# The table of TensorE durations by which a kernel orders its own instructions

## The chip, the cores and the metric

The kernel runs on one core of a Trainium2 chip. The metric is the time of one execution on the device in microseconds (us); the smaller the better. The core has a TensorE for products (PE in the profile, with PEld for its weight loads), a VectorE (DVE), a ScalarE (ACT), a GpSimd (POOL) and a SyncE (SP), each of which works off its own queue of instructions in the order in which they were put there. Products are written to banks of PSUM, everything else lies in SBUF.

## What is computed

Two blocks of a language model on x of 512 tokens by 1024 features, in fp32. What stands around the change is the first half of the first block and the window attention of the second:

```
h = rms_norm(x);  q, k, v, glu_a, glu_b = split(h @ w_in)
q, k = rms_norm over the 64 features of each of 8 heads
z = q . k / 8;  log_one_minus = where(s < t, log_sigmoid(-z), 0)
tail = reversed cumsum(log_one_minus) - log_one_minus
attn = where(s < t, exp(log_sigmoid(z) + tail), 0) @ v        # "stick breaking"
c = glu_a * sigmoid(glu_b);  c = causal depthwise convolution, 31 taps
c = silu(layer_norm(c));  x = x + concat(attn, c) @ w_out
x = x + (silu(conv3(h @ w_gate)) * (h @ w_val)) @ w_down       # 2816 wide
second block: gated linear attention (4 heads), attention in a window of 128
  with 8 heads of 64 features and 2 of keys, w_out, a feed-forward as above, rms_norm
```

## The kernel before

All operands of the large products are split into two float32r (f32r) parts, hi and lo, so that a product of fp32 accuracy is three f32r products (`mm3`): hi by hi, hi by lo, lo by hi. `WeightStream` loads the weights in chunks on SP's queue (`raw`), casts each on ScalarE (`whi25` is that of chunk 25, 128x1024) and takes the rest on VectorE (`wlo25`). The scores of both attentions are true fp32 products of 64 rows: the two heads of a pair lie in rows 0 to 63 and 64 to 127 of one tile. The trace shows an fp32 product as two records.

**The order is made by the kernel itself.** The body is written stage by stage, in the order of `ORDER1` ("glu0 glu1 k1 taps2 taps0 k0 q0 v conv0 stick0 q1 conv2 stick1 cnorm stick2 wo0 stick3 wo1 wo2 wo3") and `ORDER2`, but `rec.engine("PE")` and its like hand out proxies that only record the instruction (class `Recorder`, from line 42). `Recorder.order` (from line 154) then plays the whole program through with a table of durations, `Recorder.cost` (from line 111): an engine that comes free takes the first instruction in program order whose operands are there by then. `issue` (line 257) emits the instructions in the order of the starts thus found. So each queue's order is fixed when the kernel is built, and line 266 stands for nearly all of them in the profile. A tile belongs to a lane with a fixed number of buffers (`BUFS`), taken in program order. A copy on `ANY` goes to ScalarE or VectorE, whichever is free first in that play.

Names that return below: `q1ps0` and `q1ps1` are the two banks of the q projection of heads 4 to 7 (96 f32r products of 256 columns), `q1tn`, `q1sq`, `q1u`, `q1r` their norm on ScalarE. In `stick_pair(j)` (from line 687) heads 2j and 2j+1 have three banks of scores each (`z2_0` is head 2, bank 0): bank 0 with 256 and 128 columns, bank 1 with 384, bank 2 with 512. After the scores and a mask product, `softplus` makes `e` from a bank by Abs, Exp and Ln on ScalarE and splits it into `sph` and `spl`; products of these with triangles and blocks of -1 (`con_r`) are added onto the scores, here called sums; a last Exp from the bank gives the weights, which go into the products `av`. The convolution's first 14 taps of a pair of tiles are products by ScalarE, summed by accumulating DMAs on POOL's queue (`tap<-tap`); tap tiles share the lane x with the `e` tiles. `conv_norm` takes the mean (`cmu`) and the variance (`cvar`) by products, then `cln_u` and `crstd`, and silu in place on `conv`; its results `c_hi`, `c_lo` are the operands of the first output products `wo`. The feed-forwards (products `g`, `u`, `d`) follow. In the second block `aq` are projections for the window attention, `avT` the transposes of its values.

Of the kernel before, what the change touches and what calls it, by code (L numbers as in the profile page):

```python
# [9 lines left out]
F32R = mybir.dt.float32r  # L10
# [5 lines left out]
P = 128  # L16
# [17 lines left out]
class Op:  # L34
    """One recorded instruction."""

    def __init__(self, index, queue, method, args, kw):
        self.index, self.queue, self.method, self.args, self.kw = index, queue, method, args, kw
        self.columns = None
        self.needs, self.then, self.first, self.ready, self.end = 0, [], [], 0.0, 0.0  # L40


class Recorder:
    """Records the instructions of a kernel, orders them by list scheduling and issues them in that order.

    An engine takes, whenever it is free, the first instruction in program order whose operands are
    there; tiles of a lane are taken in program order, each when one of its buffers is free.
    """

# [6 lines left out]
    SWITCH = 40  # L56
    COPY = {"ANY": ("ACT", "DVE")}
# [56 lines left out]
    def cost(self, op, queue, out, ins):  # L114
        n = 1
        for d in out.shape[1:]:
            n *= d
        pointers = sum(1 for a in ins if a.shape[-1] == 1 and len(a.shape) == 2 and n > 1)
        op.set = None
        if op.method == "dma_start":  # L120
            op.bytes = 4 * n * out.shape[0]
            return {"SP": 450.0, "ACT": 450.0, "POOL": 1040.0}[queue]
        if queue == "PE":
            if op.method == "transpose":
                return n / 1.2 + 2
            if out.shape[0] <= 64:
                first = out.offset // out.ap[0][0]
                op.columns = frozenset(range(first, first + out.shape[0], 32))
            passes, m = (1, ins[0].shape[-1]) if ins[0].dtype == F32R else (4, 2 * ins[0].shape[-1])
            return max(passes * n / 2.4 + 2.6, m / 1.2)  # L130
        if queue == "ACT":
            func = next((a.name for a in op.args if isinstance(a, AF)), op.kw.get("func"))
            op.set = self.SETS.get(func)
            return n / 1.2 + (50 if ins[0].space == bass.MemoryType.PSUM else 93) + 93 * pointers \
                + (93 if "accum_out" in op.kw else 0)
        if queue == "POOL":
            return n / 0.96 + 60
        fast = op.method in ("copy", "tensor_copy", "tensor_scalar", "tensor_scalar_add", "tensor_scalar_mul", "memset")
        sbuf = all(a.space != bass.MemoryType.PSUM for a in [out] + ins)
        if op.method == "tensor_reduce":  # L140
            n = 1
            for d in ins[0].shape[1:]:
                n *= d
        return n / (1.92 if fast and sbuf else 0.96) + 67 + 62 * pointers

    def hop(self, a, b):
        """From the end of `a` to the earliest start of `b`, which needs it."""
# [6 lines left out]
    def order(self):  # L154
        """The instructions in the order of their starts, with the table sets to load before them."""
        free = {q: 600.0 for q in self.engines}
# [7 lines left out]
        drained, columns = 0.0, None  # L164
# [5 lines left out]
        def admit(op):  # L170
            """Operands are there: waits for its tiles, in the order of their lanes, then is offered."""
# [18 lines left out]
        while len(result) < len(self.ops):  # L190
# [35 lines left out]
            if q == "PE":  # L226
                while when >= (window + 1) * self.WINDOW:
# [41 lines left out]
class WeightStream:  # L269
    """Loads weight chunks in the order of use and splits each into two float32r parts."""  # L270
# [38 lines left out]
def weight_plan():  # L309
    """Chunks of the weights in the order of use: key, input, rows of 128 from and count, columns."""  # L310
# [87 lines left out]
def kernel(  # L398
# [70 lines left out]
    def minus_sums(src, name):  # L469
        """Minus the sums over the partitions, in each partition."""  # L470
# [7 lines left out]
    def rsqrt(ps, scale, r, name):  # L478
        """r = 1 / sqrt(scale * ps + eps): by logarithm, then one Newton step."""
# [8 lines left out]
    class Norm:  # L488
        """Parts of g * x for the products, and 1 / rms(x) by token."""
# [45 lines left out]
    def mm3(ps, w, xx, first, last):  # L535
        """ps += w.T @ x for operands given as two float32r parts each."""
# [4 lines left out]
    def project(w, m, xs, name, tag="mm"):  # L541
        """Feature-major [128 features, 512 tokens] tile m of the chunk."""
# [9 lines left out]
    def project_tok(tag, keys, xs, name):  # L552
        """Token-major [128 tokens, 512 features] tiles, all four."""
# [39 lines left out]
    cpad = []  # L593

    def glu(c):
        """By token, then by channel, with 30 zeros before the first token."""
# [39 lines left out]
    def project_quarter(keys, name, tag="mm"):  # L636
        """Token-major [128 tokens, 256 features] halves of two banks, all four."""
# [11 lines left out]
    def qk_quarter(which, c):  # L649
        """Four heads: norm over the 64 features of a head, then by feature."""  # L650
# [34 lines left out]
    BANKS = [[(2, 0), (3, 256)], [(1, 0)], [(0, 0)]]  # L685

    def stick_pair(j):
        """Two heads, scores as [s, t]: blocks of 128 positions s from the last to the first.

        log of a weight is z[s, t] - sum over s <= j < t of softplus(z[j, t]); the sums over j are  # L690
        products with triangles and blocks of -1, added to the scores where they lie.
        """
# [65 lines left out]
    def conv_taps(j0):  # L758
        """First taps of two tiles: products by ScalarE, sums by accumulating DMA."""
# [31 lines left out]
    def conv_norm():  # L791
        """Layer norm over the channels and silu."""
# [29 lines left out]
    def mixer_out(key, part, mixs, cs=range(4), norm=None, gain=None, x_in=None):  # L822
        """Columns cs; onto the tiles x_in, if given, else onto xT; norm takes the sums."""
# [71 lines left out]
    # lower bounds of the forget gates: first row of the softmax over the two rows  # L895
# [29 lines left out]
    # ================ second block ================  # L925
# [26 lines left out]
    def hg_scores(js):  # L952
        """Decayed scores q_t . k_s prod(f_{s+1..t}) of the heads js, [s, t] by tile pairs.

        ks holds k_s times the forget gates after s in its block, qp holds q_t times the gates
        of its block up to t, tot their product over each block; blocks double level by level.
        """
# [146 lines left out]
    def swa_pair(j):  # L1104
        """Two heads of one group of keys and values, side by side."""
# [36 lines left out]
        # by key: block b of itself, then block b of the next block of queries  # L1142
# [42 lines left out]
    # residual by token  # L1185
# [18 lines left out]
    def final_half(t):  # L1204
        """Sum of squares of the first half of the features; that half times its gain."""
# [7 lines left out]
    def final_part(t, cols):  # L1213
        """Adds the squares of some features of the second half."""
# [48 lines left out]
def _masks(np):  # L1263
    """Identity, level masks of the doubling, window mask; identity, triangles, blocks of -1."""
# [33 lines left out]
```

## Time and profile before

| | |
|---|---|
| runs | 1208.17, 1208.4, 1210.71 us (median 1208.4) |
| span of the profiled execution | 1205.9 us |
| median less that span | 2.5 us |
| TensorE busy | 1191.8 us, 99% |
| VectorE, ScalarE, GpSimd busy | 761.3, 504.1, 32.4 us |

The profiled execution is known by its span alone; the profile gives no other time for it. An engine is busy while it has an instruction under way; that TensorE's products follow without a gap does not say that they are needed when they run. So the table is read beside the list of waits: where TensorE waits, and what it waits for.

### The profile page before, as it was taken

The numbers are of one execution on the slowest core, as the hardware profiler recorded it, in microseconds if no ns is written. First come the engines' busy times: TensorE is split into PE (matmuls) and PEld (weight loads), VectorE is DVE, ScalarE is ACT, GpSimd is POOL, SyncE is SP. The second block draws the span as 40 slices with busy tenths as digits, with TensorE's granted clock in tenths as the row PEclk, the third lists the DMA queues.
The fourth block names the chain that finished last, engine by engine and source line by source line (L and its number), as shares of the span: only waits on it lengthen the run. The fifth ranks groups of instructions, "written<-read, shape, count | busy, mean of one in ns | idle before, by whom it ended". The sixth has DMA issues, their size and how long they took to land.

```text
span 1205.9 us, 15657 instructions
## 1 busy us (share of the span) xinstructions
PE 1191.8 (99%) x6144; PEld 988.7 (82%) x6144; DVE 761.3 (63%) x1288; ACT 504.1 (42%) x795; POOL 32.4 (3%) x85
## 2 busy tenths in 40 slices
PE   9999999999999999999999999999999999999997
PEld 8998766888888888888889877778888888888886
DVE  6889885676653566355775667877666445653554
ACT  7286796453321233133544245655523223321324
POOL 0033100000000000000000000000000000000000
PEclk9999999999999999999999999999999999999999
DMA  7389421233232323322322222112332323232321
GB/s 235 106 181 200 92 88 35 77 99 105 88 105 88 105 90 103 92 96 79 118 70 72 70 78 68 49 61 79 105 100 92 104 89 105 88 105 89 103 71 70
DMA packets 36553, 116.09 MB, mean 96 GB/s; under 512 B 4224, under 2 KB 4352, under 8 KB 36480
## 3 DMA queue, kind: packets, MB, share of 16 engines
q1 hardware_dynamic: 31248, 105.65, 28.1%
q0 software_dynamic: 4512, 8.39, 4.0%
q8 instruction: 48, 0.79, 0.3%
q10 hardware_dynamic: 720, 1.05, 0.2%
q14 instruction: 25, 0.20, 0.1%
HBM read 105.12 MB, written 2.10 MB: 89 GB/s over the span
## 4 chain that ended last, share of the span: by engine, by line
PE 94%; DMA 3%; DVE 1%; ACT 1%; issue 0%; SPq 0%; ACTq 0%; POOLq 0%
PE d L266 20%; PE g L266 20%; PE u L266 20%; PE wo L266 7%; PE z L266 4%; DMA tap<-tap 2%; PE hi L266 2%; PE glub L266 2%; PE hg L266 2%; PE glua L266 2%; PE hq L266 2%; PE hf L266 2%; PE aq L266 2%; PE hl L266 2%; PE av L266 1%; PE k0ps L266 1%
## 5 line engine op out<-in xcount | busy, mean ns | idle before, releaser
L266 ACT CAST whi<-raw 128x1024 fp32r<-128x1024 f32 (+2 forms) x194 | 200.8, 1035 | 475.2 <-PE d L266 152.1
L266 DVE TENSOR_TENSOR wlo<-raw,whi 128x1024 fp32r<-128x1024 f32 (+2 forms) x194 | 233.0, 1201 | 93.7 <-ACT whi L266 93.4
L266 PE MATMUL g<-n_hi,whi 128*128 128x512 f32 x352 | 137.2, 390 | 0.0
L266 PE MATMUL g<-n_hi,wlo 128*128 128x512 f32 x352 | 137.1, 390 | 0.0
L266 PE MATMUL g<-n_lo,whi 128*128 128x512 f32 x352 | 137.1, 389 | 0.0
L266 PE MATMUL u<-n_lo,whi 128*128 128x512 f32 x352 | 137.0, 389 | 0.0
L266 PE MATMUL u<-n_hi,whi 128*128 128x512 f32 x352 | 137.0, 389 | 0.0
L266 PE MATMUL u<-n_hi,wlo 128*128 128x512 f32 x352 | 137.0, 389 | 0.0
L266 PEld LDWEIGHTS u<-n_hi,whi 128*128 128x128 f32 x352 | 66.1, 188 | 13.8
L266 PEld LDWEIGHTS u<-n_hi,wlo 128*128 128x128 f32 x352 | 66.1, 188 | 13.7
L266 PEld LDWEIGHTS g<-n_hi,wlo 128*128 128x128 f32 x352 | 66.1, 188 | 13.7
L266 PEld LDWEIGHTS g<-n_hi,whi 128*128 128x128 f32 x352 | 66.1, 188 | 13.7
L266 PEld LDWEIGHTS u<-n_lo,whi 128*128 128x128 f32 x352 | 66.1, 188 | 13.6
L266 PEld LDWEIGHTS g<-n_lo,whi 128*128 128x128 f32 x352 | 66.1, 188 | 13.5
L266 DVE TENSOR_TENSOR s<-s,u 128x512 f32<-128x512 f32 x44 | 30.3, 688 | 67.1 <-PE u L266 67.1
L266 DVE TENSOR_TENSOR gp<-g,n__rstd 128x512 f32<-128x512 f32 x44 | 30.4, 692 | 63.9 <-PE g L266 63.8
L266 PE MATMUL d<-wlo,f_hi 128*128 128x512 f32 (+1 forms) x182 | 69.5, 382 | 0.0
L266 PE MATMUL d<-whi,f_lo 128*128 128x512 f32 (+1 forms) x182 | 69.5, 382 | 0.0
L266 PE MATMUL d<-whi,f_hi 128*128 128x512 f32 (+1 forms) x182 | 69.5, 382 | 0.0
L266 PE MATMUL d<-f_hi,whi 128*128 128x512 f32 x176 | 68.5, 389 | 0.0
L266 PE MATMUL d<-f_lo,whi 128*128 128x512 f32 x176 | 68.5, 389 | 0.0
L266 PE MATMUL d<-f_hi,wlo 128*128 128x512 f32 x176 | 68.5, 389 | 0.0
(389 smaller groups left out, 2388.6 us busy)
## 6 DMA issues: line engine op xcount, KB each, us to landing
raw<-in_weights_dram SPq DMA_DIRECT2D x182, 512.0 KB, 3.6
tap<-tap POOLq DMA_DIRECT2D x30, 256.0 KB, 4.7
raw<-in_weights_dram SPq DMA_DIRECT2D x8, 384.0 KB, 3.1
xin<-in_x_dram SPq DMA_DIRECT2D x8, 256.0 KB, 6.2
xres<-in_x_dram SPq DMA_DIRECT2D x8, 256.0 KB, 3.4
raw<-in_weights_dram SPq DMA_DIRECT2D x4, 256.0 KB, 5.7
out_dram<-hts ACTq DMA_DIRECT2D x4, 256.0 KB, 2.8
out_dram<-hts SPq DMA_DIRECT2D x4, 256.0 KB, 2.6
```

The costliest lines, as they stand in the source:

```text
L266: getattr(self.engines[op.queue], method)(*op.args, **op.kw)
```

## The change

Three things change in the durations by which `order` plays the program. An f32r product now takes 13.6 ns over its columns at 2.4 per ns (before 2.6), or 4 ns over the columns of its weights at 1.2 per ns, whichever is more; an fp32 product counts as two passes. A product of 64 rows or fewer may now stand beside another on other rows, as one with 64 outputs or fewer could before on other columns. And whenever the shape changes (64 rows or not, 64 outputs or not), 110 ns are added. Comments and docstrings went too, so that line 266 is now line 276. No operation differs.

```diff
+    DRAIN = 110.0
...
             if op.method == "transpose":
                 return n / 1.2 + 2
-            if out.shape[0] <= 64:
+            lhs = op.args[1]
+            op.shape = (lhs.shape[0] <= 64, out.shape[0] <= 64)
+            if any(op.shape):
+                first, k = lhs.offset // lhs.ap[0][0], min(lhs.shape[0], P)
+                rows = range(first, first + k, 32) if op.shape[0] else range(0, P, 32)
                 first = out.offset // out.ap[0][0]
-                op.columns = frozenset(range(first, first + out.shape[0], 32))
-            passes, m = (1, ins[0].shape[-1]) if ins[0].dtype == F32R else (4, 2 * ins[0].shape[-1])
-            return max(passes * n / 2.4 + 2.6, m / 1.2)
+                cols = range(first, first + out.shape[0], 32) if op.shape[1] else range(0, P, 32)
+                op.columns = frozenset((r, c) for r in rows for c in cols)
+            m = lhs.shape[-1] / 1.2 + 4
+            if ins[0].dtype == F32R:
+                return max(n / 2.4 + 13.6, m)
+            return 2 * max(n / 1.2 + 3, m)
...
             if q == "PE":
+                if op.shape != shape:
+                    when, shape = when + self.DRAIN, op.shape
```

**What moves.** First, TensorE's queue at the first sums of pair 0, in the middle of the q projection of heads 4 to 7; before:

```order
L266 MATMUL q1ps0_312<-whi21_274,n1_4_hi_91 128x256
L266 MATMUL q1ps0_312<-wlo21_275,n1_4_hi_91 128x256
L266 MATMUL q1ps0_312<-whi21_274,n1_4_lo_92 128x256
L266 MATMUL q1ps0_312<-whi21_274,n1_5_hi_97 128x256
L266 MATMUL z0_0_286<-sph0_0_289,con_r_121 128x128
L266 MATMUL q1ps0_312<-wlo21_275,n1_5_hi_97 128x256
```

and now:

```order
L276 MATMUL q1ps1_313<-whi20_271,n1_3_hi_88 128x256
L276 MATMUL q1ps1_313<-wlo20_272,n1_3_hi_88 128x256
L276 MATMUL q1ps1_313<-whi20_271,n1_3_lo_89 128x256
L276 MATMUL q1ps1_313<-whi20_271,n1_0_hi_73 128x256
L276 MATMUL z0_0_286<-sph0_0_289,con_r_121 128x128
L276 MATMUL q1ps1_313<-wlo20_272,n1_0_hi_73 128x256
```

The first sum (`z0_0<-sph0_0`) stood behind 64 products of `q1ps`, and stands now behind 37.

Second, TensorE's queue where the scores of pair 1 begin (`z2_*` and `z3_*` from `qn1,kn1`). Before, those of `z2_0` stand seven rows ahead of this piece:

```order
L266 MATMUL z0_2_302<-sph0_0_289,con_r_121 128x256
L266 MATMUL z0_2_302<-spl0_0_290,con_r_121 128x256
L266 MATMUL av0_285<-e0_1_296,v1_280 64x384
L266 MATMUL av0_285<-e1_1_299,v1_280 64x384
L266 MATMUL z0_2_302<-sph0_1_297,con_r_121 128x384
L266 MATMUL z0_2_302<-spl0_1_298,con_r_121 128x384
L266 MATMUL z0_2_302<-sph0_2_305,con_r_121 128x512
L266 MATMUL z3_0_335<-qn1_262,kn1_243 128x256
L266 MATMUL z0_2_302<-spl0_2_306,con_r_121 128x512
L266 MATMUL z3_0_335<-qn1_262,kn1_243 128x128
L266 MATMUL z3_0_335<-con_r_121 128x128 x2
L266 MATMUL z2_1_342<-qn1_262,kn1_243 128x384
```

and now:

```order
L276 MATMUL q1ps1_313<-whi21_274,n1_7_lo_107 128x256
L276 MATMUL z2_0_334<-qn1_262,kn1_243 128x256
L276 MATMUL z3_0_335<-qn1_262,kn1_243 128x256
L276 MATMUL z2_0_334<-qn1_262,kn1_243 128x128
L276 MATMUL z3_0_335<-qn1_262,kn1_243 128x128
L276 MATMUL z2_0_334<-con_r_121 128x128 x2
L276 MATMUL z3_0_335<-con_r_121 128x128 x2
L276 MATMUL z2_1_342<-qn1_262,kn1_243 128x384
L276 MATMUL z3_1_343<-qn1_262,kn1_243 128x384
L276 MATMUL z2_1_342<-con_r_121 128x128
L276 MATMUL z3_1_343<-con_r_121 128x128
L276 MATMUL z2_0_334<-sph2_0_337,con_r_121 128x128
```

The scores of heads 2 and 3 stood apart, in among the last sums of pair 0 (`z1_1`, `z0_2`, `z1_2`); now they stand in pairs, behind the last product of `q1ps1`, with nothing but their masks between them and their own first sums.

Third, ScalarE's queue ahead of the first Abs of head 2 (`e2_0<-z2_0`); before:

```order
L266 ACTIVATE e1_2_307<-z1_2_303 128x512
L266 COPY q1tn1_324<-q1ps1_313 128x512
L266 ACTIVATE e1_1_299<-z1_1_295 128x384
L266 CAST sph0_2_305<-e0_2_304 128x512
L266 ACTIVATE e1_2_307<-e1_2_307 128x512
L266 ACTIVATE q1sq1_326<-q1tn1_324 128x512
L266 ACTIVATE e1_2_307<-e1_2_307 128x512
L266 ACTIVATE e2_0_336<-z2_0_334 128x384
```

and now:

```order
L276 ACTIVATE e0_2_304<-z0_2_302 128x512
L276 ACTIVATE e1_2_307<-z1_2_303 128x512
L276 COPY q1tn0_323<-q1ps0_312 128x512
L276 CAST mix0_hi_310<-av0_285 128x512
L276 ACTIVATE q1sq0_325<-q1tn0_323 128x512
L276 COPY q1tn1_324<-q1ps1_313 128x512
L276 CAST whi25_408<-raw25_407 128x1024
L276 ACTIVATE q1sq1_326<-q1tn1_324 128x512
L276 ACTIVATE e2_0_336<-z2_0_334 128x384
```

The cast of weight chunk 25 (`whi25`), which stood eight instructions behind that Abs, now stands ahead of it, and so do `mix0_hi` and the last Exps of pair 0 (`e0_2<-z0_2`, `e1_2<-z1_2`). The second copy of `q1ps` from PSUM (`q1tn1`) stood six rows ahead of the Abs, and stands now three ahead, with `whi25` between.

## Rows read from the trace of the kernel before

**Rows 1.** The page: busy time of each engine, and the chain by engine.

```profile
...
PE 1191.8 (99%) x6144; PEld 988.7 (82%) x6144; DVE 761.3 (63%) x1288; ACT 504.1 (42%) x795; POOL 32.4 (3%) x85
...
PE 94%; DMA 3%; DVE 1%; ACT 1%; issue 0%; SPq 0%; ACTq 0%; POOLq 0%
...
```

**Rows 2.** Waits of TensorE: line, releaser, us in total, times, longest.

```profile
...
PE z L266 <- ACT sph L266: 2.1, 1, 2.1
...
PE avT L266 <- DVE avt L266: 1.1, 1, 1.1
...
```

**Rows 3.** The chain that ended last: start us, us, what.

```profile
...
252.80 10.88 PE u L266 x48
...
```

**Rows 4.** Windows: stretch, length, busy us of engines, PEclk, DMA share, GB/s.

```profile
...
127.20:175.60 48.40, 45.93 (x242) 29.09 (x240) 41.07 (x83) 44.49 (x93) 3.75 (x7) 1.00 0.32 78
144.50:167.50 23.00, 22.61 (x109) 13.55 (x108) 19.70 (x47) 20.69 (x47) 0.00 (x0) 1.00 0.28 92
...
177.00:241.20 64.20, 64.20 (x300) 48.06 (x299) 40.59 (x62) 37.57 (x65) 0.20 (x2) 1.00 0.20 61
241.20:601.00 359.80, 359.80 (x1589) 297.91 (x1588) 206.56 (x263) 117.32 (x140) 1.60 (x16) 1.00 0.31 97
...
```

**Rows 5.** Timeline of TensorE at pair 0: start, us, instructions, [idle <- releaser].

```profile
...
127.79 0.28 PE L266 MATMUL q1ps<-whi,n_lo 128*128 128x256 f32 x1
127.91 0.28 PE L266 MATMUL q1ps<-whi,n_hi 128*128 128x256 f32 x1
130.27 0.33 PE L266 MATMUL z<-sph,con_r 128*128 128x128 f32 x1 [2.08 <-ACT sph L266]
...
```

**Rows 6.** Timeline of ScalarE, pairs 0 to 2 and the norm.

```profile
...
127.26 0.49 ACT L266 ACTIVATE e<-z 128x384 f32<-128x384 f32 x1 [3.00 <-DMA tap<-tap]
...
143.48 0.62 ACT L266 ACTIVATE q1sq<-q1tn 128x512 f32<-128x512 f32 x1
...
144.52 0.48 ACT L266 ACTIVATE e<-z 128x384 f32<-128x384 f32 x1
...
147.76 1.04 ACT L266 CAST whi<-raw 128x1024 fp32r<-128x1024 f32 x1
...
167.51 0.69 ACT L266 ACTIVATE cln_u<-cvar,eps 128x512 f32<-128x512 f32 x1 [0.64 <-PE cvar L266]
...
175.64 2.94 ACT L266 ACTIVATE conv<-conv,prm 128x512 f32<-128x512 f32 x4
...
```

**Rows 7.** Timeline of TensorE at the scores of pair 1.

```profile
...
138.21 1.12 PE L266 MATMUL z<-qn,kn 64*128 64x512 f32 x2
...
140.61 0.92 PE L266 MATMUL z<-qn,kn 64*128 64x256 f32 x4
...
144.17 0.70 PE L266 MATMUL z<-qn,kn 64*128 64x256 f32 x2
...
145.23 0.48 PE L266 MATMUL z<-qn,kn 64*128 64x128 f32 x2
...
146.01 0.91 PE L266 MATMUL z<-qn,kn 64*128 64x384 f32 x2
146.85 0.33 PE L266 MATMUL z<-sph,con_r 128*128 128x128 f32 x1
...
148.00 0.22 PE L266 MATMUL z<-con_r 128*128 128x128 f32 x1
...
148.56 0.33 PE L266 MATMUL z<-sph,con_r 128*128 128x128 f32 x1
```

**Rows 8.** Timeline of TensorE, two score products side by side.

```profile
...
119.18 0.92 PE L266 MATMUL z<-qn,kn 64*128 64x384 f32 x4
...
```

**Rows 9.** Timeline of TensorE at the first output products.

```profile
...
177.02 0.45 PE L266 MATMUL wo<-c_hi,whi 128*128 128x512 f32 x1
...
```

**Rows 10.** Timeline of TensorE ahead of the transposes avT.

```profile
...
741.66 0.66 PE L266 MATMUL avT<-con,avt 128*128 128x128 f32 x4 [1.06 <-DVE avt L266]
...
```

**Rows 11.** Timeline of TensorE at the sums of the convolution's norm.

```profile
...
156.52 1.02 PE L266 MATMUL cmu<-cacc,ones 128*128 128x512 f32 x2
...
```

More of the change, by code (lines that the diff above doesn't have):

```diff
@@ L38, in __init__ @@
         self.index, self.queue, self.method, self.args, self.kw = index, queue, method, args, kw
-        self.columns = None
+        self.columns, self.shape = None, (False, False)
         self.needs, self.then, self.first, self.ready, self.end = 0, [], [], 0.0, 0.0
@@ L163, in order @@
         window, busy, cold = 0, 0.0, True
-        drained, columns = 0.0, None
+        drained, columns, shape = 0.0, None, (False, False)
         def offer(op):
```

## The prediction

> **What bounds the kernel now.** I began with the busy times and the chain by engine [rows 1]: TensorE has a product under way for 1191.8 of the span's 1205.9 us, and the chain that ended last runs over it for 94%. So a change that only reorders can win or lose in two ways: in the time TensorE waits, and in the time its products take beside each other. The list of its waits [rows 2] names one of weight in the first block, 2.1 us for `sph`, and one in the second, 1.1 us for `avt`.
>
> Next I looked for the stretches where that could change. In the feed-forwards TensorE is covered without a gap (359.80 of 359.80 us from 241.2 to 601), and ScalarE and VectorE are busy for 117 and 207 us of it [rows 4]: nothing in the order there can be late enough to matter, and I take nothing for either feed-forward. From the first output product (177.02) to the first `g` TensorE is covered too, 64.20 us of 64.20 [rows 4, 9]; after the attention its time is simply the work that is left. What remains is 127.2 to 177, where TensorE is busy for 45.93 of 48.40 us and ScalarE for 44.49 [rows 4]. There the two are nearly even: the reader should see that 99% for TensorE over the span doesn't make it the bound here.
>
> **The durations.** A chain piece of 48 f32r products of 512 columns takes 10.88 us [rows 3], 226.7 ns each. The table gave 215.9 ns and now gives 226.9, so in this point it now fits the trace. The Trainium skill's page TensorE: Matmul & The Clock Gate, section Back-to-back issue gap, puts such a product at 512/2.4 + about 2.5, some 216 ns, which speaks for the old entry; the trace disagrees with it by 11 ns, and by the one figure as by the other the products themselves are what they were, so that the sum is the same. A truer table is no gain in itself: what counts is where the instructions land.
>
> **Score products side by side.** One head's scores take, from start to next start, 0.84 us for 384 columns (146.01 to 146.85; the shown length is 0.07 more); less the same 0.07 it is 1.05 for 512, 0.63 for 256, 0.41 for 128, and 0.85 for 256 and 128 in one go [rows 7]. Two heads side by side take for 384 columns 0.92 less 0.07, again 0.85 [rows 8]: the second is free. In the changed order the heads of pairs 1, 2 and 3 stand together seven times where they stood apart: bank 2 three times (1.05 each), bank 1 of pair 1 (0.84), bank 0 of pair 1 (0.85+0.63+0.41-0.86 = 1.03), of pair 2 (0.61) and pair 3 (0.22, both by the same rows): 5.8 us. With each visit to the 64-row shape that falls away, the next product of full rows no longer takes its 0.33 us in place of 0.22 [rows 7]: 7 by 0.11 = 0.8. Of these 6.6 us, bank 0 and bank 2 of pair 3 lie behind the first output product, where TensorE is the bound: **-1.4 us**. The other 5.2 lie in the stretch ahead of it, and are worth something only if TensorE sets the pace there.
>
> **The opening wait.** The first sum starts at 130.27, after 2.08 us idle [rows 5]. Its head's Abs started at 127.26, after ScalarE had idled 3.00 us for the accumulating DMA of a tap tile whose buffer `e0_0` takes [rows 6]. That chain of DMAs keeps its order, so the sum stays near 130.3. But only 37 products of `q1ps` now stand ahead, not 64; at 0.120 us each (127.79 to 127.91 [rows 5]) the missing 27 lengthen the wait by 3.2 us, to about 5.3. They aren't lost: they run later. TensorE's work from 130.3 to the first output product thus changes by +3.2 - 5.2 = -2.0 us, and that is the lower bound for where it starts: 175.0.
>
> **Pair 1 starts later.** Before, pair 1's scores stood among pair 0's last sums, so ScalarE had head 2's Abs at 144.52 [rows 6], and the first sum of pair 1 ran at 148.56, with no gap in between on TensorE [rows 7]. Now they stand behind the last `q1ps1`. When is that? From 130.27 to 148.56 TensorE had 18.3 us of work. Out go pair 1's scores (0.85+0.63+0.41+0.84, with masks and changes of shape about 3.5), in come the 27 products (3.2) and pair 0's last two `av` products of 512 columns, estimated at 1.0 like a score product as wide: 19.0 us, so 149.3. ScalarE's queue then holds, in this order, the copy of `q1ps1` (about 0.5, estimated like a square of the same size less the 0.1 by which records overlap), `whi25` (1.0), the square (0.5), and only then head 2's Abs [rows 6]: with 0.2 for the hand-over **151.4, 6.9 later than before**. TensorE has no products to fill in, since the q projection is done and the output products wait for the convolution's norm: a new wait for `sph` of some 3 to 4 us.
>
> **How much of it is given back.** From that Abs to `cln_u` before lay 23.0 us (144.52 to 167.51), with ScalarE busy for 20.69 [rows 4, 6]. There are 46 instructions between them before and 47 now: `whi25`, `mix0_hi`, two last Exps and two casts have gone ahead, seven others (four `sph` casts among them) have come in, 3.4 us against 3.1 by lengths of the same forms. So `cln_u` comes at 172.2 if ScalarE doesn't idle at all, and at 174.4 at the same pace: 4.7 to 6.9 late. From `cln_u` to the first output product it is 9.5 us before (167.51 to 177.02, with silu at 175.64 [rows 6, 9]), a chain of ScalarE, VectorE and a table load; three of pair 2's and 1's ScalarE instructions (1.5 us) have left it, and if they were what it waited for, and 0.4 more of hand-overs go with them, it takes 7.6. The output products therefore start 2.8 us (no idling, shorter chain) to 6.9 us late. ScalarE still has to wait for sums at each bank, but TensorE has 5 us less to do between them; I halve its idling and leave the chain: **+5.7 us**.
>
> **The second block.** `avT` waits 1.06 us with two `aq` products of 0.23 ahead of it [rows 10]; now six stand there, 0.9 us more of cover. In two pairs of the window attention the scores of two heads now stand side by side, at most another 0.9, of which I take 0.4 since other waits of 0.3 lie beside: **-1.3 us**, with 0 and -1.8 as bounds.
>
> **The sum.** +5.7 - 1.4 - 1.3 = +3.0 us. The profiled execution's span is 1205.9; the median is 2.5 over that, for start and end that the change doesn't touch. So 1208.9 by the span, and **1211.4 us** by the median, 0.25% slower.
>
> **Rivals.**
> TensorE sets the pace all through. For it: 99% busy, and it was never idle from 130.3 to 177 by more than tenths. Against it: with scores behind the last filler it has nothing to run while `e` is made. Then the output products start 2.0 us early: -2.0 - 1.4 - 1.3, **1203.7**; and if the play lets the first sum come before the tap's DMA, so that the opening wait doesn't grow, 1200.5. It decides if pair 1's first sum comes before about 150.
> ScalarE gives back what it can: no idling and the shorter chain, +2.8 - 2.7, **1208.5**, no change. For it: pairs of heads side by side give it two independent chains. It decides if `cln_u` comes before 173.
> The norm of the convolution is later still. The sums `cmu`, which stood ahead of the first `av` of pair 1 (156.52 [rows 11]), now stand behind both bank 2 scores and an `av`; on TensorE's in-order queue they wait for all that, I follow it to 164.6, 8.1 late. If `cvar` and `cln_u` hang on this and nothing is made up, +8.1 - 2.7: **1213.8**.
>
> **How the numbers follow.** The forecast's case (output products 4.2 to 7.3 late, 1209.9 to 1213) gets 0.45, the ScalarE rival 0.22, TensorE as bound 0.2, the late norm 0.13. Within 0.2% (2.4 us, which is about what a measurement of this kernel can tell) means 1206.0 to 1210.8: all of the second case, and a quarter of the first. That makes slower 0.47, the same 0.33, faster 0.2. The range leaves out the far half of the fast case and little of the slow one: 1204.5 to 1214.3, which takes in 1 us for what I did not cost elsewhere.
>
> **What would show it.** Right: TensorE's wait for `sph` near 130 grows to about 5 us and a second of 3 to 4 us stands near 152; the first `wo` starts near 182.7; `avT` no longer waits; the visits of 64 rows to come are shorter by number, not by length. Wrong: first `wo` before 177, or ScalarE's head 2 Abs well before 151, as it would be if the last `q1ps1` product ran earlier than 149 because pair 0 didn't need the time; or a first sum before 129.

## The result, and the profile after

The changed kernel takes 1217.63 us in the median of four runs (1216.25 to 1219.65), beside 1208.29 for the kernel before (1205.1 to 1210.71). The ratio is 1.0078 [1.0057, 1.0099]: 9.4 us slower. The direction is the forecast's, the size three times its +3.0, and the time lies 3.3 us above the range.

The page of the changed kernel: busy times, the granted clock in 40 slices, the chain by engine, and the accumulating DMAs with their us from issue to landing.

```profile
span 1215.3 us, 15665 instructions
...
PE 1192.7 (98%) x6144; PEld 989.8 (81%) x6144; DVE 744.8 (61%) x1242; ACT 526.4 (43%) x841; POOL 32.4 (3%) x85
...
PEclk9999989999999999999999999999999999999999
...
PE 88%; DVE 5%; DMA 3%; ACT 3%; issue 1%; SPq 0%; POOL 0%; ACTq 0%; POOLq 0%; DVEq 0%
...
tap<-tap POOLq DMA_DIRECT2D x30, 256.0 KB, 4.9
...
```

TensorE is busy for 0.9 us more than in [rows 1] within a span 9.4 us longer. Its share of the chain falls from 94% to 88%, and VectorE and ScalarE take it over. One slice, that of 152 to 182 us, has a clock under nine tenths. The list of TensorE's waits says who is late.

```profile
PE z L276 <- ACT sph L276: 4.3, 2, 2.9
PE k0T L276 <- ACT kn L276: 3.1, 1, 3.1
...
PE k1T L276 <- DVE k1tn L276: 1.1, 1, 1.1
...
PE k1T L276 <- ACT kn L276: 0.5, 1, 0.5
```

The row for `avT` in [rows 2] is gone, as forecast. The wait for `sph` is two waits now, as forecast. But `k0T` and `k1T` (transposes in the norm of the keys, 25 to 42 us ahead of the first score) wait 4.7 us in all where they waited for nothing, and the prediction did not look there. The stretches of the changed kernel, and below them the sum for the kernel before over the same 181 us, show how much that makes.

```profile
80.00:100.00 20.00, 15.60 (x127) 14.86 (x125) 17.47 (x33) 11.87 (x20) 5.75 (x7) 1.00 0.82 174
100.00:117.00 17.00, 16.72 (x72) 13.56 (x73) 14.86 (x26) 10.54 (x18) 6.17 (x8) 0.90 0.86 171
...
150.00:160.00 10.00, 6.81 (x48) 5.31 (x47) 9.16 (x23) 8.57 (x23) 0.00 (x0) 0.98 0.33 123
160.00:170.00 10.00, 9.65 (x42) 6.07 (x42) 2.87 (x9) 4.76 (x11) 0.00 (x0) 0.68 0.16 48
170.00:180.00 10.00, 8.46 (x40) 4.78 (x39) 8.24 (x14) 9.97 (x22) 0.00 (x0) 1.00 0.11 41
180.00:190.00 10.00, 9.40 (x45) 6.11 (x44) 9.93 (x22) 9.97 (x18) 0.00 (x0) 0.83 0.09 23
...
sum 181.00, PE 169.21 PEld 132.99 DVE 132.14 ACT 126.88 POOL 26.49; mean PE 16.92 PEld 13.30 DVE 13.21 ACT 12.69 POOL 2.65
```

```profile
sum 181.00, PE 178.53 PEld 139.93 DVE 142.92 ACT 131.56 POOL 26.52; mean PE 17.85 PEld 13.99 DVE 14.29 ACT 13.16 POOL 2.65
```

From 60 to 241 us TensorE idled for 2.5 us before and idles for 11.8 now: +9.3. Besides, parts of it run at the lower clock, 1.2 GHz in place of 2.4. A stretch of length L with clock c has lost (1 - c) times L, so the rows above make 1.7 + 0.2 + 3.2 + 1.7 = 6.8 us, where before every stretch from 60 to 241 has 1.00. Against these stand the 6.6 us of the scores side by side, by the prediction's estimate. The sum, +9.5, is near what the first `g` shows: it starts 10.2 us later. This ledger says where TensorE's time went. It does not say yet what caused it, since an idle microsecond and a slow one can hide each other.

Where TensorE stands in the changed kernel, in its timeline:

```profile
100.28 0.65 PE L276 MATMUL k0T<-con,k0tn 128*128 128x128 f32 x4 [3.10 <-ACT kn L276]
...
127.64 0.34 PE L276 MATMUL q1ps<-whi,n_hi 128*128 128x256 f32 x1
...
133.68 0.33 PE L276 MATMUL z<-sph,con_r 128*128 128x128 f32 x1 [1.37 <-ACT sph L276]
...
157.94 0.44 PE L276 MATMUL z<-sph,con_r 128*128 128x128 f32 x2 [2.88 <-ACT sph L276]
...
162.51 0.52 PE L276 MATMUL z<-sph,con_r 128*128 128x384 f32 x1
...
188.74 0.40 PE L276 MATMUL wo<-c_hi,whi 128*128 128x512 f32 x1
...
251.48 0.39 PE L276 MATMUL g<-n_hi,whi 128*128 128x512 f32 x1
...
752.21 0.66 PE L276 MATMUL avT<-con,avt 128*128 128x128 f32 x4
```

The first sum comes 3.4 us later than in [rows 5], pair 1's first sum 9.4 later than in [rows 7], the first output product 11.7 later than in [rows 9]; the first `g` is 10.2 later (251.48 for 241.29) and `avT` 10.5 later than in [rows 10]. At the last product (1208.21 for 1198.82) 9.4 are left. The sum at 162.51 shows the clock by itself: 0.52 us, where a sum of the same form takes 0.34 at 1.00 (147.42 in the kernel before).

How much of the first 3.4 us is the work of the change, one trace can't tell. Experiments 8 and 11 below keep the order of the kernel before up to there, and their profiled executions have the first sum earlier than [rows 5] and later than in the changed kernel:

```profile
127.33 0.33 PE L283 MATMUL z<-sph,con_r 128*128 128x128 f32 x1 [1.28 <-ACT sph L283]
...
174.08 0.45 PE L283 MATMUL wo<-c_hi,whi 128*128 128x512 f32 x1
```

```profile
134.06 0.22 PE L283 MATMUL z<-sph,con_r 128*128 128x128 f32 x1
```

(The first two rows are 8, the third is 11.) From the first sum on the time repeats better: to the first output product it is 46.75 us before (130.27 to 177.02) and 46.75 in 8, and 55.06 in the changed kernel.

Why `k0T` waits stands on ScalarE's timeline, that of the changed kernel first (columns as before: start, length, what, idle ahead of it and its releaser).

```profile
93.66 0.72 ACT L276 ACTIVATE tap<-cpad,prm 128x512 f32<-128x512 f32 x1 [0.55 <-DMA tap<-tap]
94.29 0.57 ACT L276 COPY q0tn<-q0ps 128x512 f32<-128x512 f32 x1
98.93 0.72 ACT L276 ACTIVATE tap<-cpad,prm 128x512 f32<-128x512 f32 x1 [4.07 <-DMA tap<-tap]
99.56 0.67 ACT L276 ACTIVATE kn<-k0T,prm 128x512 f32<-128x512 f32 x1
100.12 0.62 ACT L276 ACTIVATE q0sq<-q0tn 128x512 f32<-128x512 f32 x1
100.64 0.57 ACT L276 COPY q0tn<-q0ps 128x512 f32<-128x512 f32 x1
101.11 0.70 ACT L276 ACTIVATE kn<-k0T,prm 128x512 f32<-128x512 f32 x1
```

The same place in the kernel before:

```profile
92.65 0.73 ACT L266 ACTIVATE tap<-cpad,prm 128x512 f32<-128x512 f32 x1 [0.75 <-DMA tap<-tap]
93.28 0.62 ACT L266 ACTIVATE q0sq<-q0tn 128x512 f32<-128x512 f32 x1
94.19 0.59 ACT L266 COPY q0tn<-q0ps 128x512 f32<-128x512 f32 x1 [0.30 <-PE q0ps L266]
94.68 1.05 ACT L266 CAST whi<-raw 128x1024 fp32r<-128x1024 f32 x1
95.63 0.72 ACT L266 ACTIVATE tap<-cpad,prm 128x512 f32<-128x512 f32 x1
96.25 0.69 ACT L266 ACTIVATE kn<-k0T,prm 128x512 f32<-128x512 f32 x1
...
97.84 0.69 ACT L266 ACTIVATE kn<-k0T,prm 128x512 f32<-128x512 f32 x1 [0.38 <-PE k0T L266]
```

The same tap product stands directly ahead of `kn` in both orders (98.93 and 95.63). Before, a square, a copy and the cast of a weight chunk stood ahead of it too, and when its turn came its buffer was free. Now these stand behind it, and the buffer is not free until 98.93. ScalarE, which works off its queue in order, idles 4.07 us for the accumulating DMA that holds the buffer, `kn` is late, the PSUM buffers of `k0T` stay taken, and TensorE stops for 3.1 us. The place of the three is not what makes `kn` late: ahead of the tap they would fill 2.3 us of ScalarE's wait, and the tap would still come behind the DMA. The DMA lands later, and the tap before comes later too (93.66 for 92.65); this was not followed further back. The 1.6 us at `k1T` lie ahead of it, at 83 to 86 us, and have another cause: experiment 9 below, which takes the wait at `k0T` away, keeps them.

In the play of `order` the wait looks smaller: the table has these DMAs land 650 + 262144/360 + 2000 ns = 3.4 us after their issue, while the page shows 4.9, and for the kernel before 4.7. The old table had TensorE 5% too fast beside that (215.9 ns for 226.7 [rows 3]). **Two errors of the table stood against each other at this place, and the change mended one.** Experiments 3 and 4 bear it out for the wait at `k0T`: with the old f32r entry in the opening it is 0.9 us, with a longer DMA it is gone.

### The profile page after: what moved, and what is told of

Read it like the earlier page. It is cut to its first block, busy times and chain, and to the rows that moved or that the text cites. A ratio compares the mean times of both kernels' runs of the same rounds, so it can differ in the third digit from the quotient of the medians.

```text
span 1215.3 us, 15665 instructions
## 1 busy us (share of the span) xinstructions
PE 1192.7 (98%) x6144; PEld 989.8 (81%) x6144; DVE 744.8 (61%) x1242; ACT 526.4 (43%) x841; POOL 32.4 (3%) x85
## 3 DMA queue, kind: packets, MB, share of 16 engines
q10 hardware_dynamic: 720, 1.05, 0.2%
## 4 chain that ended last, share of the span: by engine, by line
PE 88%; DVE 5%; DMA 3%; ACT 3%; issue 1%; SPq 0%; POOL 0%; ACTq 0%; POOLq 0%; DVEq 0%
PE d L276 20%; PE g L276 20%; PE u L276 20%; PE wo L276 7%; DMA tap<-tap 3%; PE z L276 3%; PE hi L276 2%; PE hg L276 2%; PE hf L276 2%; PE hq L276 2%; PE hl L276 2%; PE vps L276 2%; DVE conv L276 1%; PE av L276 1%; PE glub L276 1%; PE glua L276 1%
## 5 line engine op out<-in xcount | busy, mean ns | idle before, releaser
L276 PEld LDWEIGHTS g<-n_hi,wlo 128*128 128x128 f32 x352 | 66.1, 188 | 13.6
L276 PEld LDWEIGHTS u<-n_hi,whi 128*128 128x128 f32 x352 | 66.1, 188 | 13.6
L276 PEld LDWEIGHTS g<-n_hi,whi 128*128 128x128 f32 x352 | 66.1, 188 | 13.6
```

What stands on the lines that cost most here:

```text
L276: getattr(self.engines[op.queue], method)(*op.args, **op.kw)
```

## The experiments

Each edit is made to the changed kernel. Over before means the ratio to the kernel before, less 1, times 1208 us.

**1. The durations alone.** The products' overlap by rows, the 110 ns and the fp32 entry go back; the f32r entry stays.

```diff
-    DRAIN = 110.0
+    DRAIN = 0.0
...
-            if any(op.shape):
+            if op.shape[1]:
...
-                rows = range(first, first + k, 32) if op.shape[0] else range(0, P, 32)
+                rows = range(0, P, 32)
...
-            return 2 * max(n / 1.2 + 3, m)
+            return max(4 * n / 2.4 + 2.6, 2 * lhs.shape[-1] / 1.2)
```

> Only the f32r duration of the change (13.6 ns in place of 2.6); fp32 durations, rows and the drain as before. Theory (the truer f32r duration makes the play believe TensorE slower beside unchanged DMA times, so tap products come ahead of the norms on ScalarE's queue, and pair 1's scores behind the q projection): nearly the whole loss is here, 1215 to 1220 us, TensorE waits about 3 us at k0T, and the first output product comes 10 to 13 us late. Rival (the loss comes from the rows and the drain, which put the heads' scores side by side): within 3 us of the kernel before, no wait at k0T.

Measured: 1.0135 [1.0111, 1.0158], 16.3 us over before, more than the theory had. `k0T` waits 2.2 us, the first sum comes at 134.09, the first output product at 191.8. The one line on f32r products carries more than the whole loss.

**2. Rows and change of shape alone.** The durations go back.

```diff
-                return max(n / 2.4 + 13.6, m)
-            return 2 * max(n / 1.2 + 3, m)
+                return max(n / 2.4 + 2.6, lhs.shape[-1] / 1.2)
+            return max(4 * n / 2.4 + 2.6, 2 * lhs.shape[-1] / 1.2)
```

> Only the rows and the drain of the change; all durations as before. Theory: the tap products stand as before and TensorE doesn't wait at k0T, so 1206 to 1210 us. Rival (rows and drain make the loss): 1215 to 1219.

Measured: 1.0034 [1.0017, 1.0050], 4.1 us over. `k0T` no longer waits, the first sum comes at 129.81, the first `g` at 241.3, as before. In the profiled execution what is lost is lost in the window attention, where one stretch is at a lower clock; the kernel before has 1.00 there:

```profile
780.00:800.00 20.00, 18.83 (x76) 12.57 (x77) 14.91 (x45) 8.48 (x25) 0.00 (x0) 0.83 0.18 53
```

(1 - 0.83) times 20 is 3.4 us, and the last product of that attention comes 3.25 us later than before.

**3. The opening in its old order.** The f32r entry goes back for the products of the gates, the keys, the values and the first queries.

```diff
-                return max(n / 2.4 + 13.6, m)
+                opening = out.tensor.name.startswith(("glu", "k1ps", "k0ps", "q0ps", "vps"))
+                return max(n / 2.4 + (2.6 if opening else 13.6), m)
```

> The whole change, but the f32r products of the opening (glu, k and q of heads 0 to 3, v) keep their old duration. Theory of two losses: k0T no longer waits and the first sum comes near 130.3 again, 3.4 us earlier than in the changed kernel; pair 1's scores still stand behind the q projection, so the first output product is 5 to 8 us late, in all 1211 to 1215 us. Rival (the late pair 1 alone makes the loss, since the tap chain sets the first sum anyway): as the changed kernel, 1216 to 1219. Rival (the opening alone makes it): 1206 to 1209.

Measured: 1.0064 [1.0041, 1.0087], 7.7 us over, a little more than the theory had. `k0T` still waits 0.9 us. 63 products of `q1ps` stand ahead of the first sum, which comes at 131.45, and `wo` starts at 185.4: 3.3 us earlier than in the changed kernel, with a total only 1.7 smaller. The output products themselves run slow here:

```profile
170.00:180.00 10.00, 9.39 (x31) 4.87 (x32) 8.29 (x16) 9.91 (x20) 0.00 (x0) 0.79 0.01 2
180.00:190.00 10.00, 10.00 (x31) 6.59 (x28) 4.83 (x11) 5.79 (x9) 0.20 (x2) 0.53 0.17 52
```

From 180 to 190 TensorE is covered in full and yet at 0.53, so most of the stretch runs at 1.2 GHz.

**4. The tap DMA at its measured duration.**

```diff
-                before, after = (650, 2000) if q == "POOL" else (580, 800)
+                before, after = (650, 3300) if q == "POOL" else (580, 800)
```

> The whole change, and the play takes 1.3 us more for an accumulating DMA, so that issue to landing is about 4.7 us there, as in the trace, instead of 3.4. Theory (the old f32r duration and the old DMA time were wrong in the same direction and cancelled): no wait at k0T; all 96 products of the q projection stand ahead of the first sum, so the wait there is under 1 us and the first sum stays near 130 to 132; 1204 to 1210 us. Rival (the DMA time in the play has nothing to do with it): 1215 to 1219.

Measured: 1.0083 [1.0056, 1.0110], 10.0 us over. The wait at `k0T` is gone, but now all 96 products of `q1ps` stand ahead of the first sum, and ScalarE's queue holds a tap, both copies of `q1ps`, `whi` and two squares ahead of head 0's first Abs (136.89). The sum comes at 139.93, after 5.04 us idle, and 140 to 150 runs at 0.54. That two true entries give the best order was my theory here, and it fell: with them the play sees nothing wrong in draining TensorE's reserve of products first.

**6 and 7. In between.** The same line with 2400 and with 2700.

> The whole change, with 0.4 us more for an accumulating DMA in the play: 63 products of the q projection stand ahead of the first sum, as before the change, but the two heads of pair 1 still stand side by side behind the projection. Theory (the place of pair 1 and the clock after it make the larger loss): 1212 to 1216 us, as in the run with the opening's old durations. Rival (37 products ahead in place of 64 is the loss): 1206 to 1210.

> The whole change, with 0.7 us more for an accumulating DMA: 84 products ahead of the first sum, which fill the wait that the kernel before still had there; the scores of pair 1 stand 17 rows apart again, among pair 0's sums. Theory: wait at the first sum under 1 us, pair 1 no later than before, no half clock in the stretch: 1203 to 1209 us. Rival (any play with the true product durations loses here, by what it puts on ScalarE's queue): 1214 to 1219.

Measured: with 2400, 1.0013 [0.9998, 1.0028], 1.6 us over, and 63 products ahead of a first sum at 130.91; with 2700, 1.0049 [1.0025, 1.0072], 5.9 over, and 84 ahead of one at 132.66. With 2400 the scores of heads 2 and 3 stand together behind `q1ps`, as in the changed kernel, and head 2's Abs still comes at 147.98 in place of 154.40. So the pairing of heads needn't be dear. That the number of `q1ps` products left to run behind the first sum makes it so is my reading and not shown: 3, with 63 ahead too, loses 7.7. For 2700 I had expected less of a loss than it has.

**9. Only the tap product moved.** On ScalarE's queue the tap product named above goes behind the two `kn`; nothing else changes.

```diff
+LATE = [(('tap0_8_', 'cpad0'), ('kn1_', 'k0T1'))]
...
-            for _, op, load in sorted(self.order(), key=lambda r: r[0]):
+            queue = sorted(self.order(), key=lambda r: r[0])
+            for what, behind in LATE:
+                i, j = (next(i for i, r in enumerate(queue) if r[1].queue == "ACT"
...
+                queue.insert(max(i, j), queue.pop(i))
+            for _, op, load in queue:
```

> The changed kernel with one instruction of ScalarE's queue moved: the tap product that waited 4.07 us for its DMA stands behind kn0 and kn1 instead of ahead. Theory (the first sum is set by the tap chain, so what TensorE loses ahead of it is taken back by the wait there): k0T's wait falls from 3.1 to under 0.5 us, the q projection starts 2 to 4 us earlier, and the first sum stays within 0.7 us of where the changed kernel has it; time within 1.5 us of the changed kernel's distance to before (9.3 us), 8 to 10.8 over before. Rival (the opening wait is part of the loss): the first sum and the end come 3 us earlier, 5 to 7 over before.

Measured: 1.0046 [1.0027, 1.0065], 5.6 us over. In the trace the first `g` comes at 247.8, 3.7 us earlier than in the changed kernel. Its timeline of ScalarE, and below it the waits of TensorE and its stretches (line 284 is the line that issues):

```profile
95.55 0.69 ACT L284 ACTIVATE kn<-k0T,prm 128x512 f32<-128x512 f32 x1 [0.98 <-PE k0T L284]
...
97.42 0.69 ACT L284 ACTIVATE kn<-k0T,prm 128x512 f32<-128x512 f32 x1
98.38 0.73 ACT L284 ACTIVATE tap<-cpad,prm 128x512 f32<-128x512 f32 x1 [0.27 <-DMA tap<-tap]
...
152.39 0.86 ACT L284 ACTIVATE e<-z 128x384 f32<-128x384 f32 x2
```

```profile
PE z L284 <- ACT sph L284: 3.6, 2, 2.9
PE q0T L284 <- DVE q0tn L284: 2.1, 1, 2.1
...
PE k1T L284 <- DVE k1tn L284: 1.2, 1, 1.2
...
PE k1T L284 <- ACT kn L284: 0.7, 1, 0.7
```

```profile
150.00:160.00 10.00, 7.11 (x41) 5.90 (x39) 9.63 (x26) 8.61 (x23) 0.00 (x0) 0.76 0.44 157
160.00:170.00 10.00, 8.87 (x49) 5.19 (x48) 3.63 (x9) 6.77 (x14) 0.00 (x0) 0.90 0.18 52
```

One instruction's place, one that it had in neither order, is worth 3.8 us by the two ratios, with some 3.4 to either side, as its rival had it. From the first sum on this kernel is near the one that the prediction described: first sum at 130.78 (forecast near 130.3), last `q1ps1` at 150.1 (149.3), head 2's Abs at 152.39 (151.4), wait for `sph` of 2.9 (3 to 4). And there the output products start at 185.1, 8.0 late, where I had 5.7. The opening is not as described: the first sum waits for nothing, where I had 5.3 us, since the q projection starts at 126.29, 6.0 later than before. The waits at `k1T` (1.9 us) have stayed, and a new one of 2.1 us for `q0tn` has come up.

**10. The other instruction ahead of a first sum.** `e1_0`'s first Abs goes behind `sph0_0` on ScalarE, with `LATE = [(('e1_0_', 'z1_0'), ('sph0_0_', 'e0_0'))]` in the code of 9.

> The changed kernel with one instruction of ScalarE's queue moved: head 1's first Abs, which waited 2.20 us for a tap DMA, stands behind sph0_0 instead of ahead. Theory (its place costs at the first sum): the first sum comes 2 to 2.8 us earlier and the output products 1 to 2.5, 7 to 8.5 us over before. Rival (head 1's chain, which still waits for that DMA, sets the pace): no gain at the first output product, 9 to 10.5 over before.

Measured: 1.0068 [1.0045, 1.0091], 8.2 us over. The first sum comes 1.6 us earlier (132.10), but 130 to 140 and 140 to 150 run at 0.88 and 0.78, and `wo` starts at 191.2, 2.5 later. So the time lies in the theory's range by luck, and by time it can't be told from the changed kernel.

**5, 13 and 12. Waits filled.** To see what the clock costs, products of `con_r` that nothing reads, of 512 columns (0.227 us each at 2.4 GHz), stand where TensorE waits, so that it is busy there. In 5 they are 12 ahead of `k0T1`, 5 ahead of the first sum, 12 ahead of pair 1's first sum; in 13 the edit of 9 is made as well, with 9 ahead of `q0T0`, 3 and 12; in 12 there are 8 ahead of the first sum in the order of 11 below. They add work that the kernel does not need.

```diff
+FILLS = [(0, 'k0T1_', 'con_', 12), (0, 'z0_0_', 'sph0_0', 5), (1, 'z2_0_', 'sph2_0', 12)]
...
+                            for _ in range(n):
+                                self.engines["PE"].matmul(tile_, self.fill_by[:, 0:P], self.fill_by, start=True, stop=True)
```

> The changed kernel, with products that nothing reads put into TensorE's queue at three of its waits: 12 of 512 columns (2.7 us) ahead of k0T's second tile, 5 (1.1 us) ahead of the first sum of pair 0, 12 ahead of the first sum of pair 1. They lie inside the waits, so that the waits themselves don't change; TensorE stays active. Theory (the half clock after a wait costs as much as the wait): the granted clock stays full up to 175, the norm's cvar and the first output product come 3 to 5 us earlier than in the changed kernel, 1212 to 1215 us. Rival (ScalarE sets the pace there, so the slower products are hidden): 1216.5 to 1219, the same or a little longer.

> The changed kernel with the tap product behind kn0 and kn1, as in the run before, and products that nothing reads in the waits that are left ahead of q0T (9 of 512 columns), of the first sum (3) and of pair 1's first sum (12). Theory (two causes that add up: the tap product ahead of kn, 4.2 us, and the half clock behind the waits, 2.3 us; what is left is the later pair 1 that the prediction had priced): granted clock full from 60 to 175, 2 to 4 us over the kernel before. Rival (they are the same microseconds, since the half clock only stretched waits that the moved instruction takes away): 4.5 to 6 over before, as with the moved instruction alone.

> As the run from pair 2 on, with 8 products that nothing reads (1.8 us) in the wait of 2.1 us at the first sum. Theory (part of the spread of the kernel before, whose runs have a granted clock of 0.994 to 0.999, is a half clock behind that wait): 1 to 3 us under the run without them, and a smaller spread. Rival (the wait is too short to cost anything): the same within 0.7 us.

Measured: 5 is 1.0057 [1.0038, 1.0077], 6.9 us over, 2.4 less than the changed kernel, with some 3.5 to either side by the two intervals, and next to its rival's range; 13 is 1.0049 [1.0026, 1.0071], 5.9 over, no better than 9 without filling; 12 is 0.9985 [0.9966, 1.0004], no better than 11. In 5 the clock is 1.00 in every stretch from 60 to 241:

```profile
160.00:170.00 10.00, 8.45 (x51) 4.99 (x52) 4.04 (x13) 6.24 (x16) 0.00 (x0) 1.00 0.30 102
170.00:180.00 10.00, 8.44 (x40) 4.67 (x38) 8.56 (x16) 9.97 (x22) 0.00 (x0) 1.00 0.07 26
```

TensorE idles 1.2 us more from 160 to 170 than in the changed kernel, and from 170 ScalarE is busy to the full in both: a faster TensorE waits longer for it. Still its first output product comes 52.97 us behind its first sum (134.66 to 187.63), 2.1 less than in the changed kernel. In 13 the clock fell elsewhere (0.87 from 160 to 170, 0.67 from 180 to 190). That the edit of 9 and the fills would add up was my theory for 13, and it fell.

**8 and 11. The new table only where it pays.** A flag `second` is set at a stage, and until then `cost` uses the old entries: in 8 it is set at the second block, in 11 at pair 2 of the first attention.

```diff
+            if not self.second:
+                if out.shape[0] <= 64:
+                    first = out.offset // out.ap[0][0]
+                    op.columns = frozenset((r, c) for r in range(0, P, 32) for c in range(first, first + out.shape[0], 32))
+                passes, m = (1, ins[0].shape[-1]) if ins[0].dtype == F32R else (4, 2 * ins[0].shape[-1])
+                return max(passes * n / 2.4 + 2.6, m / 1.2)
...
+        rec.second = rec.second or step == "stick2"
```

> The change for the second block alone; the first block's order is that of the kernel before. Theory (all of the loss lies in the first block; the window attention of the second gains 1.25 us, 10.55 at avT to 9.3 at the last output product): 1.3 us less than before, 1206 to 1208.5. Rival (the gain there was bought by something before it, and the second block alone is as before or slower, as it was with rows and drain alone): 1208.5 to 1212.

> The new table only for what is recorded from pair 2 on; the opening and pairs 0 and 1 are played with the old one, so all queues are those of the kernel before until about 165 us. Theory (the loss lies in the opening and in pair 1; what stands side by side behind them and in the window attention is gained): no new wait ahead of the output products, 1.4 us less from pair 3, up to 1 from pair 2, 1.3 from the window attention: 2.7 to 3.7 us under before. Rival (the heads side by side in pair 2 make waits and half clock of their own): at or over before.

Measured: 8 is 0.9990 [0.9970, 1.0009], 1.2 us under before, which agrees with the -1.3 forecast for the second block but is within the interval of none; 11 is 0.9976 [0.9962, 0.9989], **2.9 us under before, the lowest ratio of all**, where -2.7 to -3.7 was expected.

**What the clock takes, run by run.** Each run has its mean granted clock beside its span, so (1 - clock) times the span is what it lost at the lower level. Means over the runs of a kernel, less the same for the runs of before on the same chip (for the changed kernel: for all 79 runs of before that were timed beside the experiments, 4.4 us of clock in 1208.5); the clock is recorded to 0.001, which is 1.2 us in a single run:

| kernel | runs | us over before | of it clock | the rest |
|---|---|---|---|---|
| changed | 4 | +9.3 | +5.6 | +3.6 |
| 1 durations alone | 4 | +16.2 | +6.2 | +9.9 |
| 2 rows and shape alone | 10 | +4.0 | +4.7 | -0.7 |
| 3 old opening | 5 | +8.0 | +9.1 | -1.1 |
| 4, 7, 6 tap DMA 3300, 2700, 2400 | 4, 10, 10 | +9.9, +5.2, +2.0 | +9.5, +3.9, +2.2 | +0.4, +1.3, -0.2 |
| 9 tap behind `kn` | 6 | +5.8 | +4.0 | +1.8 |
| 10 `sph` first | 4 | +9.0 | +5.9 | +3.1 |
| 5, 13 filled | 6, 7 | +6.6, +6.3 | +0.5, +1.5 | +6.2, +4.7 |
| 8 second block only | 10 | -1.6 | -0.4 | -1.2 |
| 11, 12 from pair 2 on, filled too | 12, 12 | -2.5, -1.4 | +0.7, 0.0 | -3.1, -1.4 |

By this reading nothing but the clock is lost in 2, 3, 4 and 6: their orders, at the full clock throughout, would be about as long as before. The rows of 5 and 13 show the limit of that reading: there the clock is kept up, and most of what it gives comes back as waiting and filling.

## Why the prediction was right in sign and wrong in size

**Right: the durations of the products, the feed-forwards, the second block and pair 3.** No gain came from a truer duration in itself. Between `wo` and `g` the delay falls from 11.7 to 10.2 us, so 1.5 for the forecast 1.4, which by its own rows (1.05 + 0.22 + 2 by 0.11) should have been 1.5 too. From `avT` (10.55 late) to the last product of the window attention (9.3 late, 844.53 for 835.21) it falls by 1.25, where 1.3 was forecast; counted from the first `g` it is 0.9. The feed-forward behind it changes nothing. Experiment 11 keeps these two terms, with the rest of the order nearly as before, and wins 2.9.

**Wrong: "That chain of DMAs keeps its order, so the sum stays near 130.3", and with it nothing taken for all that lies ahead of 127.2.** The DMAs keep their order on POOL's queue, but not their times, and what I did not follow is ScalarE's queue, on which the products that feed them stand, one of them ahead of `kn`. ScalarE's wait of 4.07 us for a DMA there cost TensorE 3.1 us at `k0T`, the waits at `k1T` 1.6 more, and the sum came at 133.68 (in the order of before 127.33, 130.27 and 134.06, so 3.4 us more in one trace shows little by itself). The forecast wait of 5.3 us ahead of the sum was 1.37 in turn, since the q projection began 7.3 us late (127.64 for 120.30) and head 0's Abs only 1.7 (128.93 for 127.26 [rows 6]). Experiment 9 takes the wait at `k0T` away by one instruction and wins 3.8 us, with some 3.4 to either side.

**Mis-sized: "Pair 1 starts later", +5.7.** From the first sum to the first output product, 46.75 us before, the changed kernel takes 55.06, so +8.3. Where the first sum comes when it was forecast (9) the term is +7.5 (130.78 to 185.06), and its parts up to the Abs and the wait for `sph` are as I had them within 1.1 us. What fails is what follows: "I halve its idling". ScalarE made nothing up. It did not even where the clock is 1.00 throughout: in 5 `cln_u` comes 44.65 us behind the first sum (179.31 for 134.66), where the same pace as before meant 44.1 (174.4 less 130.3). In the changed kernel it is 46.11, for TensorE, after its 2.9 us of waiting, ran part of 150 to 170 at the lower clock (0.68 from 160 to 170, where ScalarE is busy for 4.76 us of 10, and 8.81 before; in 9 0.76 and 0.90). In 5 the whole term is +6.2, so 2.1 of the 8.3 us go with the clock, by one trace of each. From 170 ScalarE is full and cannot catch up. I had read 1.00 in every row of the clock [rows 4] and carried it over to an order with new waits, without a price.

**Not forecast at all: the clock.** By the table it makes 5.6 of the 9.3 us. That much is a reading of the records, and an upper bound of what it caused; by filling the waits 2.4 came back, which isn't clear of nothing. Between these it stays open, since filling also changes who waits for whom. That in 2, 3, 4 and 6 the whole loss is clock by that reading speaks for the upper half, that filling in 13 gave nothing speaks for the lower. The play has a half clock of its own (`cold` in `Recorder.order`), which doubles its durations for TensorE in some stretches; neither the prediction nor a run asked it.

**The rivals.** TensorE as the bound fell: pair 1's first sum came at 157.94, and it had to come before 150. ScalarE giving back fell: `cln_u` came at 179.79, and it had to come before 173. The late norm is nearest: `cmu` starts at 169.2, 12.7 later than in [rows 11], where I followed it to 8.1; but it is late along with everything around it, and no run moved it alone.

Left open besides: why 2700 loses what 2400 does not. Its ten runs go from 1210.09 at a clock of 0.996 to 1222.18 at 0.985, and by the table 3.9 of its 5.2 us are clock, but what lets the clock fall there further than with 2400 was not found.

## What to carry to other kernels

A table by which a kernel orders itself is right or wrong as a whole: one truer entry can undo an error that held another in check, so look at every queue for what stands behind an instruction that waits on a DMA, ScalarE's too, and at whether that DMA still lands in time. When an order opens waits on TensorE, price the granted clock behind them too: here up to 5.6 of 9.3 us lie at the lower level. And such a table can be used by stage: from pair 2 on it gains 2.9 us, over the whole kernel it loses 9.4.

## What the runs showed of the hardware

The spread of one kernel's runs is in the main its granted clock. The 79 runs of the kernel before beside the experiments go from 1204.09 us at 0.999 to 1213.14 at 0.994, 9 us for some 6 of clock, with no instruction changed.

The lower level comes not only behind a wait of two or three microseconds. In the changed kernel it does (2.88 us of waiting, then 0.68), but in 3 the 0.53 from 180 to 190 stands behind single waits of no more than 1.3 us in the whole list, and in 2 the 0.83 in the window attention behind one of 1.1. What else decides it these runs do not show.
